# mLSTM heads of a fused block: their results copied off the accumulation bank in one piece, their transposes moved to the shared banks, the gate rows made in two steps, and compressed scores as 64-column products

## The chip, the cores and the metric

The program runs on one core of a Trainium2 chip. The metric is the time of one execution on the device, in microseconds; the median of several runs stands for a kernel. The profile is of one further execution.

## What is computed

The reference chains two transformer blocks over 512 tokens of width 1024, all in float32. Only the first block's attention stage is touched. It projects the normed input into a chunked mLSTM of four heads of width 128 and into a sparse attention ("NSA") of eight heads of width 64, which adds a compressed, a selected and a window branch:

```python
num = inter[..., None] * (qc @ Cs) + Wt @ vc
den = inter * (qc . ns) + sum(Wt)
h   = num / maximum(abs(den), exp(-m))[..., None]      # mLSTM, then rms_norm and a sigmoid gate
s_c = einsum('bgrtd,bgnd->bgrtn', qblk, Kc) - slope * dist_c
p_c = where(valid_c, softmax(s_c), 0)                  # compressed branch, 31 blocks
out = g0 * (p_c @ Vc) + g1 * o_selected + g2 * o_window
```

The gates of the mLSTM are row vectors over the 512 tokens: a cumulative sum of log sigmoids, a running maximum, and an exponential.

## The kernel before

**Arithmetic.** Each float32 operand is split into a high part and a low part (`split`, `split_w`), and a product is made of three matmuls, high x high, low x high and high x low (`mm`, L173 to L175). A weight tile is loaded by DMA (L157), its high part is cast on ACT (L137, `whi`), its low part is made on POOL in four pieces (L147, `wlo`).

**The stage.** `b1_attention` walks a string of step names, `B1_ORDER`, written out by hand. Its steps: `v`, `k`, `q0` to `q3` are the projections of the NSA; `Q`, `V`, `O` those of the mLSTM; `X`, `Y`, `B` make the compressed keys and values; `S` the compressed scores (`b1_cmp_scores`), `T` their transposes; `Ahk` the scores of head h, branch and half k, `Phk` its values, `Eh` its end; `g` the gate projections turned into rows (`b1_gates`), `R` the gate rows (`b1_mlstm_rows`); `M0` to `M3` the mLSTM heads (`b1_mlstm_head`); `W` and `u`/`U` are parts of the output projection and of a side projection that need no result of the later heads. After the stage come the splits of its results (`cat`, L212 and L213) and the rest of the output projection.

The string gives the order in which instructions are written and in which tiles take their buffers. The framework then lists the instructions of each engine in a fixed order of its own; on the chip every engine works through its list in order.

**Banks.** Eight accumulation banks: two "d" (`bankD`, dense projections and much else, tile `psd`), two "t" (transposes of the NSA, `pst`), two "s" (scores, `pss`), one "o" (values, `pso`), one "m" (`bankM`, mLSTM heads only, `psm`).

**An mLSTM head.** `b1_mlstm_head` broadcasts the running maximum through a product with a one-hot column (L1012) and copies it to `mb` (L1014). In two halves p it forms the scores k x q in bank m (L1028, by `mm`), the decay matrix E (L1032 to L1038), their product (L1042, DVE), its high part Wh (L1043, ACT) and low part Wl (L1044, POOL), and the values (L1050 with Wh, L1052 with Wl) for two token tiles, each again in bank m. Columns 0 to 127 of a result hold the low part of the numerator, 128 the denominator, 130 to 257 the high part. ACT copies the low part (L1054), DVE adds the high part out of the bank (L1055), ACT takes the absolute denominator out of the bank (L1056). Then a norm: L1058, L1059 (DVE), four squares (L1063, ACT), two POOL operations (L285, L287), L1065 and four gated scalings (L1068, DVE); each scaling is followed by a transpose on PE (L1070) into bank m, and ACT copies the four transposes (L1072).

**Compressed scores.** For a group of four heads and four token tiles, `b1_cmp_scores` makes 16 results of 32 columns; each is two accumulating products (high and low part of the keys), 32 products in one bank d (L838). One DVE addition of 512 columns adds the bias (L841).

Of the kernel before, what the change touches and what calls it, by code (L numbers as in the profile page):

```python
# [8 lines left out]
AF = mybir.ActivationFunctionType  # L9
OP = mybir.AluOpType  # L10
# [5 lines left out]
NT = 4  # L16
# [24 lines left out]
class Build:  # L41
# [402 lines left out]

    B1_SIZES = dict(k=13, v=1, pa=6, pb=2, mp=6, p2=3, f=2, mf=2, ms=2)
    B1_D = (7,)
    B1_ORDER = "C B0 v B1 Q11 k q0 q1 Q00 X0 X1 g A00 O0 Y0 V0 A10 P00 Y1 S0 A01 A02 Q01 R M0 P01 P02 T0 A03 P03 A12 q2 E0 A11 P10 A13 P11 P12 P13 A30 E1 A20 P20 A21 P21 O1 q3 A22 A23 P22 Q10 A60 P23 V1 E2 A31 S1 P30 P31 A32 T1 A33 P32 M1 c Q21 A40 A42 Q20 P33 u E3 P40 A41 P41 A43 Q30 P42 A50 P43 w E4 W0 A52 P50 A51 P51 P52 A53 P53 A61 E5 A62 Q31 W1 P60 P61 M2 M3 A70 A63 P70 P62 P63 A72 U0 A71 A73 P71 P72 P73 U1 E6 E7"

    def b1_attention(self, ctx, h, first):
        self.c1 = self.pool(ctx, "const1", 1)  # L450
        self.psum(ctx, s=2, o=1, m=1)
        self.pools(ctx, **self.B1_SIZES)
        self.qs, self.mqk, self.mv, self.mo, self.pc = {}, {}, {}, {}, {}
        self.bias, self.part, self.ob = {}, {}, {}
        self.aT, mT, x = [None] * 4, [None] * 4, {}
        for step in self.B1_ORDER.split():
            n = [int(c) for c in step[1:]]
            match step[0]:
                case "v": self.b1_v(h)
                case "k": self.b1_k(h)  # L460
                case "g": self.b1_gates()
                case "q": self.b1_q(h, *n)
                case "C": self.b1_cmp_consts()
                case "B": x["B", n[0]] = self.b1_blocks(h, n[0], first if n[0] else None)
                case "X": x["X", n[0]] = self.b1_compress(n[0], x["B", n[0]])
                case "Y": self.b1_compressed(n[0], *x["X", n[0]])
                case "S": x["S", n[0]] = self.b1_cmp_scores(*n)
                case "T": self.b1_cmp_turn(n[0], x["S", n[0]])
                case "A": self.b1_nsa_scores(*n)
                case "P": self.b1_nsa_values(*n)  # L470
                case "E": self.b1_nsa_end(*n)
                case "R": self.b1_mlstm_rows()
                case "V": self.b1_mlstm_v(h, *n)
                case "O": self.b1_mlstm_o(h, *n)
                case "Q": self.b1_mlstm_qk(h, *n)
                case "w": self.wm = self.split_all(mT[:2], "k", S)
                case "W": self.b1_out(*n)
                case "c": self.b1_conv()
                case "u": self.b1_pT()
                case "U": self.b1_pp(*n)  # L480
                case "M": mT[n[0]] = self.b1_mlstm_head(*n)
        aT = self.aT
        for i in range(4):
            self.show(f"aT{i}", aT[i])
            self.show(f"mT{i}", mT[i])
        return mT[2:] + aT
# [337 lines left out]
    def b1_cmp_scores(self, g):  # L824

        nc, a = self.nc, self.a
        cbias = self.T("f", [128, NT, 128], name="cbias")
        nc.sync.dma_start(cbias, a["c_cbias"][g])
        pc = self.T("f", [128, NT, 128], name="pcx")
        mn = self.smallE([128, NT, 4], "cmn")  # L830
        ls = self.smallE([128, NT, 4], "cls")
        s = self.bankD()
        for i in range(NT):
            for r in range(4):
                hd = 4 * g + r
                lhs = self.qs[hd // 2][:, hd % 2, i * 128:(i + 1) * 128]
                for p in range(2):
                    nc.tensor.matmul(s[:, i * 128 + r * 32:i * 128 + r * 32 + 32], lhs,  # L838
                                     self.kc[:, p, 32 * g:32 * g + 32], start=(p == 0), stop=(p == 1))
        pf = pc.rearrange("p i (r n) -> p i r n", r=4)  # L840
        nc.vector.tensor_tensor(pc, s.rearrange("p (i n) -> p i n", i=NT), cbias, op=OP.add)  # L841
        nc.vector.tensor_reduce(mn, pf, axis=AX.X, op=OP.min)
        nc.vector.tensor_tensor(pf, sub(mn, 0, 128, 0, [[4, NT], [1, 4], [0, 32]]), pf, op=OP.subtract)
        nc.scalar.activation(pc, pc, AF.Exp)
        nc.vector.tensor_reduce(ls, pf, axis=AX.X, op=OP.add)
        nc.vector.reciprocal(ls, ls)
        nc.vector.tensor_tensor(ls, ls, sub(self.gate, 0, 128, 12 * g, [[24, NT], [3, 4]]), op=OP.mult)
        nc.vector.tensor_tensor(ls, ls, sub(self.rmask, 0, 128, 0, [[1, NT], [0, 4]]), op=OP.mult)
        nc.vector.tensor_tensor(pf, pf, sub(ls, 0, 128, 0, [[4, NT], [1, 4], [0, 32]]), op=OP.mult)
        return pc  # L850
# [73 lines left out]
    def b1_mlstm_rows(self):  # L924
        nc = self.nc
        t1 = self.T("mp", [4, S], name="lf1")
        F = self.T("mp", [4, S], name="lfF")

        nc.vector.scalar_tensor_tensor(t1, self.mf, -1.0, self.mf, op0=OP.mult, op1=OP.min)
        nc.scalar.activation(t1, t1, AF.Exp)  # L930
        nc.scalar.activation(t1, t1, AF.Ln, bias=1.0)
        nc.vector.scalar_tensor_tensor(t1, self.mf, 0.0, t1, op0=OP.min, op1=OP.subtract)
        z = sub(self.zero, 0, 4, 0, [[0, S]])
        nc.vector.tensor_tensor_scan(F, t1, z, 0.0, op0=OP.add, op1=OP.add)
        A, nm = self.mi, F
        M = self.T("mp", [4, S], name="mM")
        nc.vector.tensor_sub(A, self.mi, F)
        nc.vector.tensor_tensor_scan(M, A, A, 0.0, op0=OP.max, op1=OP.max)
        nc.vector.tensor_add(nm, F, M)
        nc.scalar.activation(self.rows[32:36], nm, AF.Exp, scale=-1.0)  # L940

        self.m8 = self.C1([128, S], F32R, name="m8")
        self.zeros(self.m8, S)
        lo = self.T("f", [4, S], F32R, name="mlo")
        nc.scalar.copy(self.m8[0:4], M)
        nc.vector.tensor_sub(lo, M, self.m8[0:4].bitcast(F32))
        nc.sync.dma_start(self.m8[4:8].bitcast(F32), lo.bitcast(F32))
        oh = self.smallE([128, 4], "ohraw")
        nc.sync.dma_start(oh, self.a["c_onehot"])
        self.onehot = self.C1([128, 4], F32R, name="onehot")  # L950
        nc.scalar.copy(self.onehot, oh)
        t = self.bankD()
        for i in range(NT):
            nc.tensor.transpose(t[:, i * 128:(i + 1) * 128], self.rows[:, i * 128:(i + 1) * 128], self.ident)
        self.acol = self.C1([128, 2, NT, 4], name="acol")
        for j in range(2):
            nc.vector.tensor_copy(self.acol[:, j], sub(t, 0, 128, 32 * j, [[128, NT], [1, 4]]))
        self.tri = self.C1([128, 128], name="tri")
        nc.sync.dma_start(self.tri, self.a["c_tri"])
# [47 lines left out]
    def b1_mlstm_head(self, hd):  # L1007
        nc = self.nc
        q, k = self.mqk[hd, 0], self.mqk[hd, 1]
        v, mo = self.mv[hd], self.mo[hd]  # L1010
# [4 lines left out]
        num = self.T("mf", [128, NT, 128], name="num")  # L1015
        dn = self.smallE([128, NT], "den")
        for p in range(2):
            T0 = 256 * p
            W = []
            for jp in range(p + 1):  # L1020
                s = self.bankM().rearrange("p (b n) -> p b n", b=2)
                E, Wh, Wl = [self.T("mp", [128, 2, 256], dt, nm) for dt, nm in ((F32, "E"), (F32R, "Wh"), (F32R, "Wl"))]
                W.append((Wh, Wl))
                for b in range(2):
                    j = 2 * jp + b
# [19 lines left out]
            for i in range(2):  # L1045
                ti = 2 * p + i
                o = self.bankM()
                cs = slice(128 * i, 128 * i + 128)
                for j in range(ti + 1):
                    nc.tensor.matmul(o[:, :258], W[j // 2][0][:, j % 2, cs], v[:, j], start=(j == 0), stop=False)  # L1050
                for j in range(ti + 1):
                    nc.tensor.matmul(o[:, 128:258], W[j // 2][1][:, j % 2, cs], v[:, j, 128:], start=False, stop=(j == ti))  # L1052
                lo = self.T("ms", [128, 128], name="nlo")
                nc.scalar.copy(lo, o[:, :128])  # L1054
                nc.vector.tensor_add(num[:, ti], o[:, 130:258], lo)  # L1055
                nc.scalar.activation(dn[:, ti:ti + 1], o[:, 128:129], AF.Abs)  # L1056

        nc.vector.tensor_tensor(dn, dn, self.acol[:, 1, :, hd], op=OP.max)  # L1058
        nc.vector.reciprocal(dn, dn)  # L1059
# [3 lines left out]
            nc.scalar.activation(sc, num[:, ti], AF.Square, scale=dn[:, ti:ti + 1], accum_out=ss[:, ti:ti + 1])  # L1063
        r = self.rstd(ss, MD, [128, NT])
        nc.vector.tensor_mul(r, r, dn)  # L1065
        t = self.bankM()
        for ti in range(NT):
            nc.vector.scalar_tensor_tensor(num[:, ti], num[:, ti], r[:, ti:ti + 1],  # L1068
                                           mo[:, ti], op0=OP.mult, op1=OP.mult)
# [733 lines left out]
```

## Time and profile before

| | before |
|---|---|
| runs, median | 1648.41 us (1645.42 to 1650.79, 3 runs) |
| profiled execution, own time | 1646.16 us |
| its span, first to last instruction | 1644.1 us |
| granted TensorE clock, mean | 0.981 |
| PE busy | 1559.4 us (95%) |
| PE weight loads | 1381.5 us (84%) |
| DVE busy | 962.1 us (59%) |
| ACT busy | 763.5 us (46%) |
| POOL busy | 511.5 us (31%) |
| chain of waits: share of PE / DVE / ACT / DMA / POOL | 76% / 9% / 4% / 4% / 3% |

The stage of the change runs from about 48 us to 333 us of the span. How to read the views: a row of the timeline gives start, duration, engine, line, operation and tile; in brackets stand the engine's idle time before it and what released it. A row of stretches gives the busy time of each engine in that stretch with the number of instructions, then the granted TensorE clock as a share of full speed (1.00 is 2.4 GHz, 0.50 is 1.2 GHz), the DMA share and GB/s. Matmuls overlap: one that lasts 0.28 us can be followed by the next after 0.11 us.

### The profile page before, as it was taken

The numbers are of one execution on the slowest core, as the hardware profiler recorded it, in microseconds if no ns is written. First come the engines' busy times: TensorE is split into PE (matmuls) and PEld (weight loads), VectorE is DVE, ScalarE is ACT, GpSimd is POOL, SyncE is SP. The second block draws the span as 40 slices with busy tenths as digits, with TensorE's granted clock in tenths as the row PEclk, the third lists the DMA queues.
The fourth block names the chain that finished last, engine by engine and source line by source line (L and its number), as shares of the span: only waits on it lengthen the run. The fifth ranks groups of instructions, "written<-read, shape, count | busy, mean of one in ns | idle before, by whom it ended". The sixth has DMA issues, their size and how long they took to land.

```text
span 1644.1 us, 25907 instructions
## 1 busy us (share of the span) xinstructions
PE 1559.4 (95%) x9702; PEld 1381.5 (84%) x9702; DVE 962.1 (59%) x2158; ACT 763.5 (46%) x1727; POOL 511.5 (31%) x645
## 2 busy tenths in 40 slices
PE   6999998889999999899899999999999998999997
PEld 5889977778888888789898899998798887988785
DVE  4486667745444434658866558535468548566453
ACT  4465656734333223545554446433445445554332
POOL 4663533131111112326432243012555340431022
PEclk9999989989999999999999999999999999999999
DMA  5532222455333333322122144135323231332252
GB/s 173 139 106 68 66 78 78 151 184 165 91 101 91 102 110 110 103 89 78 39 74 66 54 117 129 40 105 170 127 62 90 59 89 35 106 115 87 77 180 76
DMA packets 189376, 163.60 MB, mean 100 GB/s; under 512 B 9664, under 2 KB 161312, under 8 KB 189252
## 3 DMA queue, kind: packets, MB, share of 16 engines
q1 hardware_dynamic: 189252, 161.96, 32.7%
q8 instruction: 76, 1.25, 0.3%
q14 instruction: 48, 0.39, 0.1%
HBM read 139.19 MB, written 12.58 MB: 92 GB/s over the span
## 4 chain that ended last, share of the span: by engine, by line
PE 76%; DVE 9%; ACT 4%; DMA 4%; POOL 3%; issue 3%; SPq 0%; POOLq 0%; ACTq 0%; DVEq 0%
PE psd L173 14%; PE psd L174 13%; PE psd L175 13%; PE pss L173 7%; PE pss L174 7%; PE pss L175 7%; POOL wlo L147 1%; PE pss L1447 1%; DMA wraw<-in_w_in_dram 1%; ACT whi L137 1%; PE pst L1472 1%; PE pso L1484 1%; PE pss L1585 1%; DVE pt L202 1%; PE pst L1608 1%
## 5 line engine op out<-in xcount | busy, mean ns | idle before, releaser
L147 POOL TENSOR_TENSOR wlo<-wraw,whi 128x256 fp32r<-128x256 f32 (+1 forms) x384 | 284.4, 772 | 369.1 <-ACT whi L137 353.2
L137 ACT CAST whi<-wraw 128x1024 fp32r<-128x1024 f32 (+2 forms) x215 | 210.9, 982 | 337.3 <-PE psd L174 81.7
L173 PE MATMUL psd<-hh,whi 128*128 128x264 f32 (+2 forms) x1016 | 340.6, 336 | 3.3 <-ACT sg L1671 1.3
L175 PE MATMUL psd<-hh,wlo 128*128 128x264 f32 (+2 forms) x1016 | 338.3, 333 | 0.5 <-DVE wlo L140 0.5
L174 PE MATMUL psd<-hl,whi 128*128 128x264 f32 (+2 forms) x1016 | 338.8, 334 | 0.0
L140 DVE TENSOR_TENSOR wlo<-wraw,whi 128x1024 fp32r<-128x1024 f32 (+1 forms) x118 | 131.2, 1112 | 206.6 <-ACT whi L137 206.5
L173 PEld LDWEIGHTS psd<-hh,whi 128*128 128x128 f32 x1016 | 193.1, 190 | 22.8 <-ACT sg L1671 1.6
L175 PEld LDWEIGHTS psd<-hh,wlo 128*128 128x128 f32 x1016 | 193.2, 190 | 18.3 <-DVE wlo L140 1.0
L174 PEld LDWEIGHTS psd<-hl,whi 128*128 128x128 f32 x1016 | 193.3, 190 | 17.1
L173 PE MATMUL psd<-whi,hh 128*128 128x256 f32 (+1 forms) x480 | 136.6, 286 | 5.1 <-ACT mo L359 2.3
L175 PE MATMUL psd<-whi,hl 128*128 128x256 f32 (+1 forms) x480 | 135.6, 283 | 0.0
L174 PE MATMUL psd<-wlo,hh 128*128 128x256 f32 (+1 forms) x480 | 135.2, 283 | 0.0
L173 PEld LDWEIGHTS psd<-whi,hh 128*128 128x128 f32 x480 | 90.0, 188 | 6.7 <-ACT mo L359 2.5
L330 POOL TENSOR_TENSOR y<-x,g 128x512 f32<-128x512 f32 (+1 forms) x34 | 48.2, 1431 | 145.2 <-DVE x L522 103.2
L201 ACT CAST pt<-pst 128x512 fp32r<-128x512 f32 (+3 forms) x130 | 63.7, 506 | 61.5 <-PE pst L1472 48.1
L202 DVE TENSOR_TENSOR pt<-pst,pt 128x512 fp32r<-128x512 f32 (+3 forms) x130 | 74.7, 583 | 27.9 <-ACT pt L201 27.3
L175 PEld LDWEIGHTS psd<-whi,hl 128*128 128x128 f32 x480 | 90.3, 188 | 0.1
L174 PEld LDWEIGHTS psd<-wlo,hh 128*128 128x128 f32 x480 | 90.2, 188 | 0.2
L1115 POOL TENSOR_TENSOR act<-conv,act 128x512 fp32r<-128x512 f32 x16 | 25.4, 1587 | 161.9 <-ACT act L1114 161.9
L1455 DVE TENSOR_REDUCE gls<-pss 128x1 f32<-128x528 f32 (+1 forms) x66 | 46.5, 704 | 33.8 <-PE pss L1447 33.2
L300 ACT ACTIVATE sq<-x 128x512 f32<-128x512 f32 (+1 forms) x58 | 36.3, 627 | 59.7 <-DVE x L1243 31.5
L175 PE MATMUL pss<-hh,wlo 128*128 128x512 f32 x160 | 63.3, 395 | 0.0
(472 smaller groups left out, 3656.4 us busy)
## 6 DMA issues: line engine op xcount, KB each, us to landing
wraw<-in_w_in_dram SPq DMA_DIRECT2D x108, 512.0 KB
wraw<-in_w_up_dram SPq DMA_DIRECT2D x32, 512.0 KB
wraw<-in_w_out_dram SPq DMA_DIRECT2D x24, 512.0 KB
wraw<-in_w_down_dram SPq DMA_DIRECT2D x16, 512.0 KB
nbias<-in_na_bias_dram SPq DMA_DIRECT2D x16, 408.0 KB
k<-k SPq DMA_DIRECT2D x16, 296.0 KB
wraw<-in_w_ple_gate_dram SPq DMA_DIRECT2D x8, 512.0 KB
x_mid<-x SPq DMA_DIRECT2D x8, 512.0 KB
```

The costliest lines, as they stand in the source:

```text
L137: nc.scalar.copy(hi, raw)
L140: nc.vector.tensor_sub(lo, raw, hi.bitcast(F32))
L147: nc.gpsimd.tensor_sub(lo[:, p[0], p[1]], raw[:, p[0], p[1]], hi[:, p[0], p[1]].bitcast(F32))
L173: m(ps, A[0], B[0], start=start, stop=False)
L174: m(ps, A[0], B[1], start=False, stop=False)
L175: m(ps, A[1], B[0], start=False, stop=stop)
L201: nc.scalar.copy(hi, src)
L202: nc.vector.tensor_sub(lo, src, hi.bitcast(F32))
L300: nc.scalar.activation(sq[:x.shape[0], :x.shape[1]], x, AF.Square, scale=scale, accum_out=ss)
L330: self.nc.gpsimd.tensor_tensor(y[:n, c], x[:, c], g[:n, c], op=OP.mult)
L1115: nc.gpsimd.tensor_sub(lo, u, hi.bitcast(F32))
L1455: nc.vector.tensor_reduce(mx, sv, axis=AX.XY, op=OP.max, negate=True)
```

## The change

Four edits:

- **Result copies.** ACT copies all 258 columns of a head's result to the tile `nlo` at once; the DVE addition and the absolute value read the copy instead of the bank.
- **Transposes.** The four transposes at a head's end go into a bank d instead of bank m.
- **Gate rows.** The step `g` moves to just behind `B1`, the step `R` to just behind `k`, and the last part of `R` (transposes of the rows into columns, `acol`, and the load of `tri`) becomes a step `r` ahead of `S0`.
- **Compressed scores.** Each product now takes the high and low keys side by side, 64 columns; 16 products for a group instead of 32, in two banks d of eight products each. DVE adds the first half with the bias and then the second half, 256 columns each, for each bank.

```diff
-    B1_ORDER = "C B0 v B1 Q11 k q0 q1 Q00 X0 X1 g A00 O0 Y0 V0 A10 P00 Y1 S0 A01 A02 Q01 R M0 P01 P02 T0 ...
+    B1_ORDER = "C B0 v B1 g Q11 k R q0 q1 Q00 X0 X1 A00 O0 Y0 V0 A10 P00 Y1 r S0 A01 A02 Q01 M0 P01 P02 T0 ...
...
+                case "r": self.b1_mlstm_columns()
...
-        s = self.bankD()
-        for i in range(NT):
-            for r in range(4):
-                hd = 4 * g + r
-                lhs = self.qs[hd // 2][:, hd % 2, i * 128:(i + 1) * 128]
-                for p in range(2):
-                    nc.tensor.matmul(s[:, i * 128 + r * 32:i * 128 + r * 32 + 32], lhs,
-                                     self.kc[:, p, 32 * g:32 * g + 32], start=(p == 0), stop=(p == 1))
+        rows = lambda t, b: t[:, 2 * b:2 * b + 2].rearrange("p i (r n) -> p (i r) n", r=4)
+        for b in range(2):
+            s = self.bankD()
+            for j in range(8):
+                i, hd = 2 * b + j // 4, 4 * g + j % 4
+                nc.tensor.matmul(s[:, 64 * j:64 * j + 64].rearrange("p (q n) -> p q n", q=2),
+                                 self.qs[hd // 2][:, hd % 2, i * 128:(i + 1) * 128],
+                                 self.kc[:, :, 32 * g:32 * g + 32], start=True, stop=True)
+            sv = s.rearrange("p (j q n) -> p j q n", j=8, q=2)
+            nc.vector.tensor_tensor(rows(pc, b), sv[:, :, 0], rows(cbias, b), op=OP.add)
+            nc.vector.tensor_tensor(rows(pc, b), sv[:, :, 1], rows(pc, b), op=OP.add)
...
-        nc.vector.tensor_tensor(pc, s.rearrange("p (i n) -> p i n", i=NT), cbias, op=OP.add)
...
+
+    def b1_mlstm_columns(self):
+        nc = self.nc
         t = self.bankD()
...
-                lo = self.T("ms", [128, 128], name="nlo")
-                nc.scalar.copy(lo, o[:, :128])
-                nc.vector.tensor_add(num[:, ti], o[:, 130:258], lo)
-                nc.scalar.activation(dn[:, ti:ti + 1], o[:, 128:129], AF.Abs)
+                lo = self.T("ms", [128, 258], name="nlo")
+                nc.scalar.copy(lo, o[:, :258])
+                nc.vector.tensor_add(num[:, ti], lo[:, 130:258], lo[:, :128])
+                nc.scalar.activation(dn[:, ti:ti + 1], lo[:, 128:129], AF.Abs)
...
-        t = self.bankM()
+        t = self.bankD()
```

The rest of the string is as it was, and no arithmetic outside these functions changes. The order of the instructions on the engines changes throughout the stage. Three places:

**PE, the first head's end (M0).** Names: `mv,Wh` and `mv,Wl` are the values of a head, `mq` its scores, `hh` dense projections, `pt,v` and `k,qs` the NSA, `ident,num` the head's transposes. Before, around the head's four transposes:

```order
L1070 MATMUL psm<-ident,num 128x128
L173 MATMUL psd<-whi,hh 128x256
L174 MATMUL psd<-wlo,hh 128x256
L1070 MATMUL psm<-ident,num 128x128
L175 MATMUL psd<-whi,hl 128x256
L1070 MATMUL psm<-ident,num 128x128
L173 MATMUL psd<-whi,hh 128x256
L174 MATMUL psd<-wlo,hh 128x256
L1070 MATMUL psm<-ident,num 128x128
L175 MATMUL psd<-whi,hl 128x256
```

Dense projections stand between the transposes, as between all of the head's steps. After the change (line numbers of the new file: 1057 and 1059 are the values, 1019 the broadcast for the next head, 1077 the transposes, 860 the transposes of the compressed scores), from the scores of the head's second half on:

```order
L173 MATMUL psm<-mq 128x128
L174 MATMUL psm<-mq 128x128
L175 MATMUL psm<-mq 128x128
L1057 MATMUL psm<-mv,Wh 128x258 x3
L1059 MATMUL psm<-mv,Wl 128x130 x3
L1057 MATMUL psm<-mv,Wh 128x258 x4
L1059 MATMUL psm<-mv,Wl 128x130 x4
L1019 MATMUL psm<-m_743,onehot 128x512
L1077 MATMUL psd<-ident,num 128x128
L860 MATMUL psd<-ident,pcx 128x128 x4
L1077 MATMUL psd<-ident,num 128x128 x3
L920 MATMUL pso<-pct,vc 128x512
```

No dense projection and no product of the NSA stands any more between the head's first scores and its transposes.

**DVE, the same head.** Before, from the division (L1058, L1059) to the gated scalings:

```order
L1058 TENSOR_TENSOR den<-den,acol 128x4
L1059 RECIPROCAL den<-den 128x4
L879 ISA sb,mn<-pss_2191,abias 128x128
L879 ISA mn 128x1
L879 ISA sb,mn<-pss_2196,abias 128x256
L879 ISA mn 128x1
L205 SCALAR_TENSOR_TENSOR qlo<-psd,qs 64x512
```

After the change the same place on DVE (1065, 1066 the division, 1042 the next head's decay matrix, 1072 and 1075 the scalings):

```order
L1049 TENSOR_TENSOR E<-psm,E 128x128
L1062 TENSOR_TENSOR num<-nlo 128x128 x2
L1065 TENSOR_TENSOR den<-den,acol 128x4
L1066 RECIPROCAL den<-den 128x4
L1042 SCALAR_TENSOR_TENSOR E<-mb,acol,tri 128x128 x2
L1072 TENSOR_TENSOR rstd<-rstd,den 128x4
L1075 SCALAR_TENSOR_TENSOR num<-num,rstd,mo 128x128 x4
L202 TENSOR_TENSOR pct<-psd,pct 128x512
L205 SCALAR_TENSOR_TENSOR qlo<-psd,qs 64x512
L926 TENSOR_TENSOR aT<-pso,aT 64x512
L205 SCALAR_TENSOR_TENSOR qlo<-psd,qs 64x512
L360 TENSOR_SCALAR mo<-mo 128x128
```

The work of other steps that stood between is gone from there.

**PE, the end of the stage.** Before, the last values of the NSA and of the head M3, then the rest of the output projection (`cat`):

```order
L1052 MATMUL psm<-mv,Wl 128x130 x4
L907 MATMUL psd<-pt,v 128x256 x3
L907 MATMUL psd<-pt,v 128x128
L916 MATMUL psd<-pct,vc 128x512 x2
L1070 MATMUL psm<-ident,num 128x128 x4
L173 MATMUL pss<-whi,cat 128x512
```

After the change:

```order
L1077 MATMUL psd<-ident,num 128x128
L911 MATMUL psd<-pt,v 128x128
L911 MATMUL psd<-pt,v 128x256 x3
L911 MATMUL psd<-pt,v 128x128
L920 MATMUL psd<-pct,vc 128x512 x2
L173 MATMUL psd<-whi,pT 128x512
```

The 48 products of the side projection (`pT`) that were spread over the last two heads now stand in one piece behind M3's transposes and ahead of `cat`.

## Rows read from the trace of the kernel before

**Rows 1.** The page: busy time of PE, its share of the span, instructions.

```profile
PE 1559.4 (95%) x9702; PEld 1381.5 (84%) x9702; DVE 962.1 (59%) x2158; ACT 763.5 (46%) x1727; POOL 511.5 (31%) x645
```

**Rows 2.** Stretches of the stage: length, PE, PEld, DVE, ACT, POOL, clock, DMA.

```profile
48.00:144.00 96.00, 91.98 (x571) 81.58 (x571) 61.83 (x159) 52.22 (x125) 59.09 (x82) 0.96 0.42 115
144.00:190.00 46.00, 45.80 (x312) 42.10 (x313) 27.20 (x87) 26.96 (x81) 25.14 (x38) 1.00 0.27 78
...
248.00:297.00 49.00, 44.12 (x265) 37.13 (x263) 39.49 (x116) 32.98 (x94) 14.85 (x20) 1.00 0.30 103
297.00:333.00 36.00, 28.69 (x175) 24.43 (x175) 23.42 (x70) 24.58 (x70) 5.17 (x7) 0.94 0.47 162
```

**Rows 3.** Timeline of PE around the first head and its gate rows.

```profile
104.25 0.38 PE L173 MATMUL psd<-whi,hh 128*128 128x256 f32 x1 [2.26 <-ACT mo L359]
...
144.20 0.38 PE L173 MATMUL psm<-mq 128*128 128x256 f32 x1 [0.60 <-ACT mb L1014]
...
189.23 0.27 PE L1070 MATMUL psm<-ident,num 128*128 128x128 f32 x1
...
190.15 0.27 PE L1070 MATMUL psm<-ident,num 128*128 128x128 f32 x1
```

**Rows 4.** Groups by form: the head's operations, mean ns behind the comma.

```profile
L1042 DVE TENSOR_TENSOR E<-psm,E 128x256 f32<-128x256 f32 x8 | 3.3, 418 | 0.5 <-PE psm L175 0.4
...
L1042 DVE TENSOR_TENSOR E<-psm,E 128x512 f32<-128x512 f32 x4 | 2.8, 690 | 5.5 <-PE psm L175 5.5
...
L1054 ACT COPY nlo<-psm 128x128 f32<-128x128 f32 x16 | 4.3, 268 | 5.5 <-PE psm L1052 5.3
...
L1043 ACT CAST Wh<-E 128x256 fp32r<-128x256 f32 x8 | 3.3, 408 | 3.8 <-DVE E L1042 3.8
...
L1014 ACT COPY mb<-psm 128x512 f32<-128x512 f32 x4 | 2.4, 596 | 0.7 <-PE psm L1012 0.7
...
L1044 POOL TENSOR_TENSOR Wl<-E,Wh 128x256 fp32r<-128x256 f32 x8 | 6.1, 764 | 23.7 <-ACT Wh L1043 23.6
L1044 POOL TENSOR_TENSOR Wl<-E,Wh 128x512 fp32r<-128x512 f32 x4 | 5.3, 1322 | 36.9 <-ACT Wh L1043 28.3 <-PE psd L174 8.6
```

**Rows 5.** Timeline of all engines at the last head's end.

```profile
323.63 0.56 PE L1052 MATMUL psm<-mv,Wl 128*128 128x130 f32 x4
...
324.49 1.22 DVE L140 TENSOR_TENSOR wlo<-wraw,whi 128x1024 fp32r<-128x1024 f32 x1 [1.60 <-ACT whi L137]
...
330.96 1.17 PE L1070 MATMUL psm<-ident,num 128*128 128x128 f32 x4 [5.79 <-DVE num L1068]
...
333.32 0.79 PE L173 MATMUL pss<-whi,cat 128*128 128x512 f32 x1 [1.19 <-ACT cat L212]
```

**Rows 6.** Short stretches, columns as in rows 2.

```profile
132.00:137.00 5.00, 5.00 (x18) 4.41 (x18) 4.88 (x12) 2.14 (x6) 0.33 (x1) 0.50 0.39 108
...
206.00:212.00 6.00, 6.00 (x31) 6.00 (x30) 5.90 (x15) 2.56 (x8) 2.23 (x5) 0.50 0.34 113
...
325.00:331.00 6.00, 0.21 (x2) 0.07 (x1) 2.65 (x9) 2.40 (x10) 1.20 (x2) 0.81 0.74 266
...
333.00:339.00 6.00, 5.68 (x14) 4.48 (x15) 3.70 (x6) 2.87 (x6) 0.00 (x0) 0.51 0.49 175
```

**Rows 7.** Groups by form: scores out of their bank, first and last of four widths.

```profile
L879 DVE CUSTOM_DVE_ANT_0 sb<-pss,abias 128x512 f32<-128x512 f32 x16 | 10.9, 682 | 0.0
...
L879 DVE CUSTOM_DVE_ANT_0 sb<-pss,abias 128x128 f32<-128x128 f32 x16 | 4.6, 286 | 9.4 <-PE pst L901 5.7 <-PE pss L878 3.5
```

**Rows 8.** Timeline of PE: 64-column products, and the compressed scores twice.

```profile
126.44 0.28 PE L174 MATMUL psd<-w,grep 128*128 128x64 f32 x1
126.55 0.28 PE L175 MATMUL psd<-w,grep 128*128 128x64 f32 x1
...
127.97 4.51 PE L838 MATMUL psd<-kc,qs 128*128 128x32 f32 x32
...
203.45 4.70 PE L838 MATMUL psd<-kc,qs 128*128 128x32 f32 x32
```

More of the change, by code (lines that the diff above doesn't have):

```diff
@@ L446 @@
     B1_D = (7,)
-    B1_ORDER = "C B0 v B1 Q11 k q0 q1 Q00 X0 X1 g A00 O0 Y0 V0 A10 P00 Y1 S0 A01 A02 Q01 R M0 P01 P02 T0 A03 P03 A12 q2 E0 A11 P10 A13 P11 P12 P13 A30 E1 A20 P20 A21 P21 O1 q3 A22 A23 P22 Q10 A60 P23 V1 E2 A31 S1 P30 P31 A32 T1 A33 P32 M1 c Q21 A40 A42 Q20 P33 u E3 P40 A41 P41 A43 Q30 P42 A50 P43 w E4 W0 A52 P50 A51 P51 P52 A53 P53 A61 E5 A62 Q31 W1 P60 P61 M2 M3 A70 A63 P70 P62 P63 A72 U0 A71 A73 P71 P72 P73 U1 E6 E7"
+    B1_ORDER = "C B0 v B1 g Q11 k R q0 q1 Q00 X0 X1 A00 O0 Y0 V0 A10 P00 Y1 r S0 A01 A02 Q01 M0 P01 P02 T0 A03 P03 A12 q2 E0 A11 P10 A13 P11 P12 P13 A30 E1 A20 P20 A21 P21 O1 q3 A22 A23 P22 Q10 A60 P23 V1 E2 A31 S1 P30 P31 A32 T1 A33 P32 M1 c Q21 A40 A42 Q20 P33 u E3 P40 A41 P41 A43 Q30 P42 A50 P43 w E4 W0 A52 P50 A51 P51 P52 A53 P53 A61 E5 A62 Q31 W1 P60 P61 M2 M3 A70 A63 P70 P62 P63 A72 U0 A71 A73 P71 P72 P73 U1 E6 E7"
     def b1_attention(self, ctx, h, first):
```

## The prediction, made before the changed kernel ran

> **What bounds the kernel now.** I read four views. The page first: PE is busy 95% of the span [rows 1], so the reader is to see that only two things can move the time, PE's own work and the places where PE stands still or runs slowly. Then the stretches between the landmarks of the stage [rows 2], the column of PE beside the length: from 144 to 190 us, where the first mLSTM head runs, PE is busy 45.80 of 46.00 us, although that head needs one bank for a long chain over four engines. Its last four transposes come at 189 to 190 us [rows 3], 45 us after its first product, and nobody waits for them, because dense projections fill PE. The stretches around the later heads are looser: 44.12 of 49.00 and 28.69 of 36.00 us. The timeline at the last head's end [rows 5] shows why: no dense work is left, PE waits 5.79 us for the norm, then 1.19 us for the split of the result. Last, the clock [rows 6]: after the products of 32 columns it is at 0.50 from 132 to 137 us and from 206 to 212 us, with PE busy throughout, and at 0.51 from 333 to 339 us, after the idle end of the last head.
>
> **The change part by part.** All sums are against the profiled execution, 1646.16 us, whose span is 1644.1 us; it lies 2.25 us under the median of 1648.41 us, and I carry the difference over to the median.
>
> *Bank of the transposes, first head: the large cost.* A head's transposes now take a bank d, and banks d are given out in the order of the program. T0, q2 and what follows come behind M0 in that order, so they get a bank d only once M0's first transpose has its own, at the very end of the chain. The order shows the result: between the first scores of M0 and its transposes PE has nothing else, nor has DVE, while before dense products stood between. So M0's chain, hidden before, is bare. Its idle time on PE, hop by hop: first product of E with the scores 0.42, high part 0.41, low parts on POOL 0.76 and about 0.5 for the narrower one [rows 4]: 2.1 us. Three copies of 258 columns, each ahead of the next use of bank m; the trace has 0.27 us for 128 and 0.60 for 512 columns [rows 4], so about 0.38, with the passing on of each 0.45: 1.35 us. The 512-wide product of E between the two score tiles: 0.69 us. The last pair again 2.1 us, more if POOL is still at the 512-wide low part of 1.32 us [rows 4]: 2.7. The end, from the last value to the first transpose, as for M3: 323.63 + 0.56 to 330.96, 6.8 us, less the 1.22 us in which DVE made a weight's low part first [rows 5]: 5.6. Three more transposes (0.9 us apart first to last [rows 3]) and a copy of 0.6 until the next projection has a bank: 1.5. Sum 13.9, say 14 us; the wait before the first product (0.60 us [rows 3]) stays. Bounds: 10 if the pieces overlap, 18 if each hop pays more.
>
> Ahead of M0, the gate columns, both additions of the scores, their softmax, eight small splits of the compressed values, three evictions and four scalings stand on DVE before the low part that M0's scores need: by rows of 0.29 to 0.69 us [rows 4, 7] some 14 us, against 24 dense products at 0.235 us and 35 short ones at 0.11 us, 9.5 us, on PE: 4 us more (0 to 5). After such a halt the clock is low: 6 us at 0.51 behind M3's end [rows 6] lost about 3 us of products. The same behind M0: 3 us.
>
> *Bank of the transposes, second head.* Behind V1 the next dense projections (Q21, Q20) need a bank d after M1's transposes. The order leaves there only NSA steps and M1: on PE 28 score products, 33 transposes, 38 values, 16 compressed scores and 35 products of M1, at 0.11 to 0.23 us about 20.5 us; on DVE eleven evictions, ten scalings and ten splits of mean width, about 0.5 us each (between 0.29 and 0.68 [rows 7]), 16 us, M1's own 6.6 and the second softmax 4.3, together 27 us. DVE ends last: 6 us (bounds 2 and 9).
>
> *End of the stage.* The side projection's 48 products (0.235 us each, 11.3 us) now follow M3 and cover its end and the splits: the idle 5.79 + 1.19 us [rows 5] and the slow clock behind it go. But they no longer fill the last two heads: there DVE has some 24.5 us against 14 us on PE. New: 24.5 + 11.3 + 1 = 37 us; old: 297 to 333.3 us [rows 2, 5] and some 2.6 us lost to the slow clock [rows 6], 39 us. Net -2 us (bounds -8 and +5). Behind M1, Q21 and Q20 come in one piece and out of the looser stretch; of its 4.9 idle us [rows 2] I give half back: -2.5 us.
>
> *Compressed scores.* 32 products took 4.51 and 4.70 us [rows 8], partly at half clock. Products of 64 columns follow each other after 0.11 us [rows 8], so 16 take 1.8 us: -2.7 and -2.9 us. The slow stretches behind them (5.0 us and about 4 us at 0.50 [rows 6]) go if the clock stays up: 2.5 + 2.0 us. I take -9 us of 10.1, since a part falls where DVE ends last; if the clock falls all the same, -5. Four additions of about 0.42 us each instead of one of 0.69 add 1 us of DVE per group, counted in the sums of DVE above.
>
> *Copies and gate rows.* The 16 copies of 258 columns instead of 128 add 0.11 us each on ACT, which is busy 46%: nothing beyond the hops above. The release of bank m comes one DVE addition earlier, which counts only where bank m ends last. The early gate rows take the Exp, Ln and cumulative sums away from the place where PE waited 2.26 us for ACT [rows 3]; what is late next there is DVE, so -2 us. At their new place PE has the broadcast for M0 in its list behind 72 projection products (17 us) and would stand if the rows were later than that. Bounds -2 and +5.
>
> Sum: 14 + 4 + 3 + 6 - 2 - 2.5 - 9 - 2 = +11.5 us: 1657.7 us for a profiled execution, 1660 us for the median.
>
> **A rule against this sum.** What the trace shows of one bank m is the chain of M3 [rows 5]: values, copy, norm, transposes, 6.8 us in which the bank is held. The Trainium skill, page "Perfetto Trace Analysis", section "Optimizing Tensor Performance", says that independent groups of matmuls should rotate through different banks so that the evacuation of one overlaps the products of the next. By that rule, moving the transposes to the pair of banks d is a gain; the sum would be that of the first rival. No row here has a head's transposes in a bank d.
>
> **The rivals.**
>
> *Faster: the heads overlap after all.* If half the bare chain is hidden (7 us in place of the 21 for chain, wait ahead and clock), M1 costs 2 and the end is worth its full -9 us: 7 + 2 - 9 - 2.5 - 9 - 2 = -13.5 us, 1635 us. For it: the idle end of M3 and the slow clock are real and the new order removes them. Against it: the lists of all engines at M0 hold M0 alone. It decides at an idle time of PE in M0 of less than about 5 us.
>
> *No difference.* M0 at its lower bound (10 + 0 + 2), M1 3, the rest as above: 12 + 3 - 15.5 = about 0, 1648 us.
>
> *Much slower: the gate rows come late.* The rows' chain (two cumulative sums, Exp, Ln, about 13 us, then a DMA and the product of it) is behind PE's 17 us in good order only if ACT and DVE reach it at once; every later microsecond stops the whole of PE, as its list has the broadcast ahead of the projections of q0 and q1. With 8 us there: 1668 us. Against it: ACT and DVE are busy only 52.22 and 61.83 of 96 us in that stretch [rows 2].
>
> *It does not do what it says.* Excluded by the order: copies of 258 columns, transposes into `psd`, 64-column products are all there.
>
> **How the numbers follow.** About 0.3%, 5 us, is what a measurement of this kernel can tell from no change. The forecast of 1660 us has 0.52, much slower 0.13: slower 0.65. No difference 0.16. Faster 0.19. The range leaves out about half of the fastest rival and the tail above the slowest: 1635 to 1675 us. It takes in M0 from 10 to 18 us, M1 from 2 to 9, the scores from -10 to -5.
>
> **What would show it.** A stretch of about 20 us around M0 in which PE is busy less than half, with the first transpose waiting more than 4 us for DVE; the same more weakly behind V1, with DVE near full; then no idle time before the first product of `cat`; a clock of 1.00 through the 64-column products. The prediction is wrong if PE stays above 90% through M0, or if the clock falls at the 64-column products too, or if PE stands at the broadcast in the gate rows.

## The result and the profile after

The changed kernel takes 1670.84 us (median of 4 runs, 1667.96 to 1672.69) against 1648.49 us in runs of the kernel before on the same chip: ratio 1.0137, 95% interval 1.012 to 1.0153. It is 22.4 us slower. The forecast was 1660 us, 11.5 us slower, with a range of 1635 to 1675: the side was right, the loss twice the forecast.

The page of the changed kernel, its busy times (compare [rows 1]):

```profile
span 1670.6 us, 25857 instructions
## 1 busy us (share of the span) xinstructions
PE 1572.1 (94%) x9670; PEld 1388.2 (83%) x9670; DVE 964.6 (58%) x2164; ACT 770.5 (46%) x1727; POOL 513.7 (31%) x645
```

The stretches of the kernel before, from 48 us to the first product of `cat`, and from there to the end (length; then busy time of PE, PEld, DVE, ACT, POOL; clock; DMA):

```profile
48.00:333.32 285.32, 265.35 (x1650) 234.00 (x1650) 189.59 (x554) 168.55 (x467) 123.45 (x172) 0.96 0.34 103
333.32:1644.10 1310.78, 1260.77 (x7850) 1118.34 (x7850) 751.48 (x1560) 573.83 (x1208) 367.58 (x442) 0.99 0.32 97
```

The same of the changed kernel, and its stretches around the first head (137 to 171 us, compare [rows 2]) and the last two (318 to 362 us):

```profile
48.00:361.33 313.33, 277.46 (x1619) 238.84 (x1616) 190.30 (x559) 172.65 (x465) 125.97 (x171) 0.91 0.29 86
361.33:1670.60 1309.27, 1259.84 (x7850) 1118.47 (x7850) 753.12 (x1560) 576.04 (x1208) 367.14 (x442) 0.99 0.33 99
...
137.00:150.00 13.00, 11.56 (x45) 9.61 (x45) 8.52 (x29) 4.33 (x11) 1.62 (x3) 0.74 0.15 42
150.00:171.00 21.00, 12.18 (x45) 9.75 (x45) 5.91 (x21) 8.97 (x31) 6.40 (x10) 0.52 0.09 25
171.00:230.00 59.00, 58.16 (x399) 53.24 (x398) 31.83 (x98) 29.08 (x74) 23.49 (x35) 0.97 0.23 61
...
318.00:345.00 27.00, 20.50 (x115) 16.77 (x115) 20.52 (x65) 15.71 (x50) 3.67 (x5) 0.82 0.12 40
345.00:362.00 17.00, 13.35 (x59) 10.35 (x58) 3.84 (x5) 9.08 (x15) 0.00 (x0) 0.99 0.53 179
```

Read the two pairs against each other first. Behind the stage nothing is lost (1309.27 against 1310.78 us). The stage is 28.0 us longer, of which PE's idle time is 15.9 us (313.33 - 277.46 = 35.9 against 20.0) and its busy time 12.1 us, although it has some thirty products fewer: they run at a lower mean clock, 0.91 against 0.96. So nearly half of the stage's loss is not waiting but slow products.

PE's timeline in the first head (brackets: idle time before, and what ended it; L1057 and L1059 are the values, L1061 the copy, L1049 the product with E, L1019 the broadcast for the next head, L1077 the transposes):

```profile
151.82 0.58 PE L1057 MATMUL psm<-mv,Wh 128*128 128x258 f32 x1 [1.01 <-ACT Wh L1050]
...
153.56 0.80 PE L1057 MATMUL psm<-mv,Wh 128*128 128x258 f32 x2 [0.47 <-ACT nlo L1061]
...
157.58 0.58 PE L173 MATMUL psm<-mq 128*128 128x256 f32 x1 [0.78 <-DVE E L1049]
...
159.91 1.01 PE L1057 MATMUL psm<-mv,Wh 128*128 128x258 f32 x3 [0.78 <-DVE E L1049]
161.92 1.23 PE L1057 MATMUL psm<-mv,Wh 128*128 128x258 f32 x4 [0.47 <-ACT nlo L1061]
164.36 0.79 PE L1019 MATMUL psm<-m,onehot 128*128 128x512 f32 x1 [0.47 <-ACT nlo L1061]
169.18 0.47 PE L1077 MATMUL psd<-ident,num 128*128 128x128 f32 x1 [4.02 <-DVE num L1075]
```

Each hop of the chain stands as a wait of PE, with no dense product (`whi,hh`) between. Before, this head lay hidden in 45.80 busy of 46.00 us [rows 2].

The end of the stage, PE and then ACT (compare [rows 5]; `pp` is the side projection, L649 ACT's copies of its results, L212 the split that `cat` needs):

```profile
339.88 0.48 PE L1077 MATMUL psd<-ident,num 128*128 128x128 f32 x1 [1.66 <-DVE num L1075]
...
346.10 0.40 PE L173 MATMUL psd<-whi,pT 128*128 128x512 f32 x1
...
357.28 0.40 PE L175 MATMUL psd<-whi,pT 128*128 128x512 f32 x1
361.33 0.51 PE L173 MATMUL pss<-whi,cat 128*128 128x512 f32 x1 [3.65 <-ACT cat L212]
```

```profile
345.09 0.59 ACT L1079 COPY mo<-psd 128x512 f32<-128x512 f32 x1 [6.25 <-PE psd L1077]
...
356.43 0.60 ACT L649 ACTIVATE pp<-psd 128x512 f32<-128x512 f32 x1 [0.85 <-DMA p_proj<-pp]
357.71 1.05 ACT L137 CAST whi<-wraw 128x1024 fp32r<-128x1024 f32 x1 [0.68 <-PE psd L175]
360.17 0.60 ACT L649 ACTIVATE pp<-psd 128x512 f32<-128x512 f32 x1 [1.41 <-DMA p_proj<-pp]
360.66 1.13 ACT L212 CAST cat<-mo 128x512 fp32r<-128x512 f32 x2
```

The 48 products of the side projection run behind the last head in one piece, 346.10 to 357.68 us, 11.6 us against the 11.3 of the prediction. They stand behind the head's transposes (339.88 us and later), so they cover nothing of the wait ahead of those. And ACT has the eight copies of their results ahead of the split in its list; the last of them waits for a transfer of `pp`. PE waits 3.65 us for the split where it waited 1.19 before.

### The profile page after: what moved, and what is told of

The parts are those of the page before. It is cut to its first block, busy times and chain, and to the rows that moved or that the text cites. A ratio compares the mean times of both kernels' runs of the same rounds, so it can differ in the third digit from the quotient of the medians.

```text
span 1670.6 us, 25857 instructions
## 1 busy us (share of the span) xinstructions
PE 1572.1 (94%) x9670; PEld 1388.2 (83%) x9670; DVE 964.6 (58%) x2164; ACT 770.5 (46%) x1727; POOL 513.7 (31%) x645
## 4 chain that ended last, share of the span: by engine, by line
PE 71%; DVE 9%; DMA 3%; ACT 3%; issue 2%; POOL 1%; SPq 0%; POOLq 0%; ACTq 0%; DVEq 0%
PE psd L173 13%; PE psd L175 12%; PE psd L174 12%; PE pss L173 6%; PE pss L175 6%; PE pss L174 6%; PE pss L1454 2%; PE pst L1479 1%; PE pso L1491 1%; DVE pt L202 1%; PE pss L1592 1%; DMA wraw<-in_w_out_dram 1%; ACT whi L137 1%; PE pst L1615 1%; DVE wlo L140 1%
## 5 line engine op out<-in xcount | busy, mean ns | idle before, releaser
L147 POOL TENSOR_TENSOR wlo<-wraw,whi 128x256 fp32r<-128x256 f32 (+1 forms) x384 | 288.4, 782 | 401.6 <-ACT whi L137 381.3
```

The lines of the kernel that those rows point to most:

```text
L147: nc.gpsimd.tensor_sub(lo[:, p[0], p[1]], raw[:, p[0], p[1]], hi[:, p[0], p[1]].bitcast(F32))
```

## The experiments

Twelve kernels ran beside the changed one. Ratios are to the kernel before, run on the same chip in the same set. Its own median was 1648.4 to 1651.2 us in these sets, so a difference of two medians from different sets is uncertain by 2 to 3 us; where it is small, the ratios decide.

| kernel | median us | ratio (95% interval) |
|---|---|---|
| changed kernel | 1670.84 | 1.0137 (1.012 to 1.0153) |
| all but the bank | 1642.82 | 0.9970 (0.9958 to 0.9983) |
| bank alone | 1695.87 | 1.0296 (1.0280 to 1.0311) |
| scores alone | 1645.10 | 0.9983 (0.9971 to 0.9995) |
| gate rows alone | 1650.01 | 1.0009 (0.9998 to 1.002) |
| first head in d | 1659.66 | 1.0064 (1.0042 to 1.0086) |
| three later heads in d | 1655.28 | 1.0049 (1.0031 to 1.0066) |
| last head in d | 1647.20 | 0.9994 (0.9981 to 1.0007) |
| second head in d | 1641.92 | 0.9953 (0.9935 to 0.9972) |
| bank and copies | 1680.08 | 1.0192 (1.0169 to 1.0215) |
| first head in d, written late | 1647.41 | 0.9987 (0.9975 to 1.0000) |
| first and second in d, late | 1656.03 | 1.0047 (1.0029 to 1.0066) |
| copies and scores | 1640.85 | 0.9949 (0.9931 to 0.9967) |

**All but the bank.** The changed kernel with one line put back:

```diff
-        t = self.bankD()
+        t = self.bankM()
```

> The change with the four transposes of a head back in bank m; copies, gate rows and 64-column scores stay. Theory A (the bank of the transposes cost more than the 22.5 us that the prediction gave it, and the other three parts gave the forecast 11 us): about 1637 us (1633 to 1642), and PE busy over 90% through the first head. Theory B (the bank cost what was forecast, and the other parts gave nothing): about 1648 us (1645 to 1652). Theory C (one of the other parts costs time itself): over 1653 us.

Measured: 1642.82 us. That lies between theories A and B: the bank costs 28.0 us, more than the 22.5 of theory B, and the other three parts gain 5.8 us, half of the 11 of theory A. The sign of theory A is there: from 140 to 186.4 us, in the first head, PE is busy 45.74 of 46.40 us. The stage, and the last head's transposes:

```profile
48.00:327.43 279.43, 260.54 (x1618) 227.92 (x1617) 188.35 (x558) 171.34 (x466) 126.08 (x171) 0.98 0.32 96
```

```profile
314.57 0.59 PE L1077 MATMUL psm<-ident,num 128*128 128x128 f32 x2
```

With the same products, the stage of the changed kernel has 17.0 us more idle time (35.9 against 18.9) and 16.9 us more busy time (277.46 against 260.54). These are two single executions, 32.2 us apart where the medians are 28.0 apart. The last head's transposes wait for nothing here: the 5.79 us of [rows 5] are gone without bank d.

**Bank alone.** The kernel before with `bankM` made `bankD` in that line.

> The kernel before with one edit, the four transposes of a head in a bank d. Theory A: about 1680 us (1675 to 1688), as this part is the whole loss and 11 us of gain are missing beside it. Theory B: about 1671 us (1667 to 1674). Theory C: below 1664 us. In all three PE has less than 60% busy in a stretch of some 20 us around the first head; the clock there is at 0.50 under theory A for 25 us or more.

Measured: 1695.87 us, 47.3 us slower, beyond all theories. What all three had in common is there: from 150 to 170 us PE is busy 11.63 of 20.00 us. So the parts don't add: beside the other three the bank costs 28. The next kernel takes a part of this apart.

**Bank and copies.** The kernel before with the bank and with the copies of 258 columns.

> The kernel before with the transposes in a bank d and the copies of 258 columns. With the bank alone it took 1695.9 us, and PE waited 0.88 us at each release of bank m in the bare heads where the changed kernel waited 0.47. Theory H (the copies pay by these hops alone, at most 4 x 0.41 us in each of four heads): 1689 to 1695 us. Theory K (the copies also bring the rest of the 25 us between the bank alone and the whole change, by another order of the work): 1671 to 1680 us.

Measured: 1680.08 us, so the copies bring 15.8 us here, and theory K stands nearer; it also asked where. The stage and what follows, of the bank alone and then of bank and copies:

```profile
48.00:372.94 324.94, 286.90 (x1651) 249.26 (x1651) 187.95 (x553) 170.38 (x467) 123.84 (x171) 0.89 0.28 82
372.94:1693.20 1320.26, 1266.21 (x7850) 1123.41 (x7850) 751.25 (x1560) 575.46 (x1208) 369.27 (x442) 0.98 0.33 98
```

```profile
48.00:361.06 313.06, 283.00 (x1655) 246.03 (x1653) 186.75 (x554) 173.56 (x467) 124.98 (x172) 0.91 0.30 88
361.06:1681.90 1320.84, 1264.95 (x7850) 1122.61 (x7850) 755.02 (x1560) 574.16 (x1208) 365.56 (x442) 0.98 0.32 97
```

With the copies the stage is as long as in the changed kernel (313.06 against 313.33 us), although this profile and that of the bank alone have a slow clock from 84 to 104 us that cost some 6 us and that the changed kernel's lacks (last section). What is left between these two profiles lies behind the stage: 1320.84 against 1309.27 us, in code that no edit touches. The order of PE's products there differs from kernel to kernel; that this order costs the time is not shown, and the four runs of bank and copies spread over 7 us. In the bank alone PE waits at bank m for the read of the denominator,

```profile
151.85 0.58 PE L173 MATMUL psm<-mq 128*128 128x256 f32 x1 [0.88 <-ACT den L1056]
...
159.04 1.23 PE L1050 MATMUL psm<-mv,Wh 128*128 128x258 f32 x4 [0.88 <-ACT den L1056]
```

0.88 us a release against 0.47 with the copies. Four such hops in a head are 1.6 us; the rest of the 11.9 us in the stage is not told apart.

**Which head.** The changed kernel with bank d for some heads only:

```diff
-        t = self.bankD()
+        t = (self.bankD() if hd in (0,) else self.bankM())
```

and `(1, 2, 3)`, `(3,)` and `(1,)` in place of `(0,)`.

> The changed kernel with the transposes of the first head alone in a bank d, those of the other three back in bank m. With all four back in bank m it took 1642.8 us, with all four in d 1670.8, so the bank costs 28 us there. Theory A (the first head is the loss, 21 us by the prediction and the rest of the 28 too): 1664 to 1670 us. Theory D (the later heads hold most of it): 1650 to 1657 us.

> The changed kernel with the first head's transposes back in bank m and those of the other three heads in a bank d. Theory A: 1643 to 1648 us, since by the prediction's sum the second head costs 6 us and the end gives 4.5 back. Theory D: 1655 to 1663 us, since the second and third heads lose their dense products as the first did and the end gives nothing back.

> The changed kernel with the last head's transposes alone in a bank d. By the prediction's term for the end (the side projection's products cover the wait of 5.8 us and the split behind it, with the slow clock after it): 1635 to 1639 us against 1642.8 with bank m throughout. By theory D (what the side projection fills at the end is missing in the last two heads, where DVE ends last, and the split is late all the same): 1643 to 1650 us.

> The changed kernel with the transposes of the second head alone in a bank d. The three later heads together cost 12.5 us (1655.3 against 1642.8 us with bank m throughout), the last alone 4.4, so 8 us are left for the second and the third. By the prediction's term the second costs 6 us: 1647 to 1651 us. If the loss is the third head's, which the prediction had as a gain of 2.5 us: 1641 to 1645 us. If it lies in both only together: 1644 to 1647 us.

Measured against 1642.82 us with bank m throughout: first head +16.8 us, three later heads +12.5, together 29.3, about the 28.0 of all four. So these two add, and neither theory holds whole: the first head is the larger loss, but less than A had, and the later heads lose where A had them near nothing. Of them the last costs 4.4 us alone, as theory D had it and against a forecast gain; but in the kernel that it is compared with the wait that bank d was to remove is gone already. The second costs nothing that can be measured (-0.9 us, by the ratios -3, their intervals overlapping; forecast +6). That leaves about 9 us for the third head, or for the third with the others; the third alone wasn't run.

Where the 12.5 us lie, from the broadcast for the second head to the first product of `cat`, with bank m throughout and then with three later heads in d:

```profile
192.43:327.43 135.00, 122.43 (x747) 105.10 (x746) 97.70 (x312) 89.99 (x261) 40.55 (x54) 0.99 0.28 91
195.13:344.03 148.90, 130.16 (x747) 109.88 (x745) 99.41 (x313) 90.29 (x261) 40.02 (x54) 0.93 0.25 84
```

The stretch is 13.9 us longer with the same 747 products: PE is idle 6.2 us more, and the products take 7.7 us more at the lower clock.

**Order or sharing.** The gated scalings, the four transposes and their copy of the first head are written as a step of their own, `m0`, behind `q3`; in the second kernel also those of the second head, `m1`, behind `Q20`.

```diff
-... E0 A11 ... O1 q3 A22 ... Q21 A40 A42 Q20 P33 ...
+... E0 A11 ... O1 q3 m0 A22 ... Q21 A40 A42 Q20 m1 P33 ...
...
+                case "m": mT[n[0]] = self.b1_mlstm_turn(*mT[n[0]])
```

> As the kernel with the first head's transposes alone in a bank d (1659.7 us, against 1642.8 with bank m), but its gated scalings and transposes are written later in the program, behind the step q3, so that T0, q2, O1 and q3 get their banks d first; the other heads stay in bank m. Theory A (the loss is the order in which banks d are given out, and not the sharing of the banks): 1642 to 1648 us, PE busy over 90% through the first head. Theory S (the head's transposes in the pair of banks d delay the dense projections wherever they are written): 1653 to 1661 us.

> As the kernel before it in this set, with the second head treated alike: its transposes in a bank d, written behind the step Q20, so that Q21 and Q20 get their banks first. Theory A: 1641 to 1649 us, within 4 us of the kernel with the first head alone. Theory S: 5 us or more above that one. If a head's end in another bank than m really frees the next head: 3 us or more below it, under 1640 us.

Measured: 1647.41 us with the first head, so of its 16.8 us 12.2 go when only the place in the program changes, with the same bank. Theory A holds for it, its sign too (PE busy 38.89 of 40.00 us). The stretch of the first head, in the kernel with the first head in d and then written late:

```profile
150.00:190.00 40.00, 32.10 (x176) 27.89 (x177) 13.99 (x44) 17.25 (x53) 9.10 (x15) 0.74 0.14 36
```

```profile
150.00:190.00 40.00, 38.89 (x261) 34.86 (x261) 19.76 (x56) 22.89 (x61) 20.75 (x33) 1.00 0.24 67
```

261 products instead of 176, at full clock. With the second head also late the time is 1656.03 us, 8.6 us more, against theory A; but the profile places it behind the stage, not in the heads. The part from the first product of `cat` on, with the first head late and then with both:

```profile
338.75:1645.40 1306.65, 1257.52 (x7850) 1115.81 (x7850) 755.01 (x1561) 574.13 (x1208) 368.19 (x442) 0.99 0.33 99
```

```profile
335.49:1651.50 1316.01, 1260.56 (x7850) 1119.94 (x7850) 751.52 (x1561) 574.29 (x1208) 368.81 (x442) 0.98 0.33 98
```

9.4 us more there, again in untouched code and for a reason not found. The two stages are 290.75 and 287.49 us, and only the first of these profiles has the slow clock from 84 to 104 us. So this kernel says nothing sure for or against theory S in the second head.

**Scores alone.** The kernel before with the 64-column products and their four additions.

> The kernel before with one edit, the compressed scores as 64-column products in two banks. Theory A (the edit gives what the prediction took): about 1639 us (1637 to 1644), the clock at 1.00 in the 6 us behind the products. Theory B (the clock falls behind the 64-column products as it did behind those of 32, or what is won there waits for DVE): 1645 to 1649 us.

Measured: 1645.10 us, a gain of 3.5 us: theory B's end. Where the rest went, on PE and in the stretches behind the first and the second group:

```profile
134.00 1.76 PE L838 MATMUL psd<-kc,qs 128*128 128x64 f32 x8 [1.61 <-DVE ls L895]
```

```profile
132.00:134.00 2.00, 0.39 (x3) 0.03 (x1) 1.52 (x6) 0.89 (x3) 2.00 (x3) 1.00 0.86 250
134.00:136.00 2.00, 2.00 (x10) 2.00 (x11) 1.72 (x6) 0.41 (x2) 0.76 (x1) 0.53 0.83 230
...
206.00:208.00 2.00, 2.00 (x20) 1.95 (x19) 1.78 (x7) 2.00 (x8) 2.00 (x4) 1.00 0.01 4
208.00:210.00 2.00, 1.92 (x14) 1.50 (x13) 2.00 (x7) 1.32 (x6) 2.00 (x4) 1.00 0.58 158
210.00:212.00 2.00, 0.84 (x4) 0.40 (x4) 2.00 (x8) 1.18 (x4) 0.63 (x2) 1.00 0.35 123
...
216.00:218.00 2.00, 1.53 (x8) 1.50 (x8) 2.00 (x8) 0.44 (x2) 0.51 (x2) 0.51 0.04 12
```

The products themselves are short, and through the second group the clock holds at 1.00. But PE then stands still behind DVE: 1.61 us ahead of the first group's second half, and from 210 us on, where DVE is busy 2.00 of every 2.00 us. Only then does the clock fall. What was a slow clock with PE busy [rows 6] is now a wait for DVE with the slow clock behind it.

**Gate rows alone.** The kernel before with the new places of `g`, `R` and `r`.

> The kernel before with one edit, the gate rows in two steps with the new places of g, R and r. Theory A: about 1646 us (1644 to 1649), the wait of 2.26 us for the running maximum gone and nothing late in its place. Theory C (the early rows push work of DVE and ACT into a place where PE waits): 1652 us or more.

Measured: 1650.01 us, ratio 1.0009 with 1 in its interval: no measurable change, where -2 us was forecast, and below the 1652 of theory C. The wait of 2.26 us [rows 3], for the output gate `mo` that ACT reached only after the gates' two functions, goes. At the early place of the gates PE waits instead, and from 48 to 72 us its clock is 0.86 where it was 1.00 before:

```profile
48.62 0.60 PE L664 MATMUL psd<-ident,gi 128*4 128x128 f32 x4 [0.77 <-ACT rows L665]
51.07 0.80 PE L173 MATMUL psd<-hh,whi 128*128 128x512 f32 x1 [1.85 <-DVE v L202]
```

**Copies and scores.** The kernel before with these two edits.

> The kernel before with two edits, copies of 258 columns and 64-column scores; gate rows and bank of the transposes as before. If the parts add up (all three but the bank 1642.8 us, gate rows alone 1.4 us slower): 1639 to 1643 us, and the copies are worth 3 to 5 us beside the scores alone at 1645.1. If the copies give nothing where the heads are covered, as the prediction has it: 1644 to 1647 us.

Measured: 1640.85 us, ratio 0.9949: the fastest kernel of the study beside the one with the second head in d (0.9953; their intervals overlap). The copies are worth 4.3 us beside the scores, as the first expectation had it. The last head's transposes in the scores alone, and the end of this kernel, where they wait for nothing and side-projection products stand between them:

```profile
331.25 1.17 PE L1073 MATMUL psm<-ident,num 128*128 128x128 f32 x4 [5.80 <-DVE num L1071]
```

```profile
314.45 0.59 PE L1073 MATMUL psm<-ident,num 128*128 128x128 f32 x2
314.99 0.50 PE L173 MATMUL psd<-whi,pT 128*128 128x512 f32 x1
...
316.49 0.38 PE L1073 MATMUL psm<-ident,num 128*128 128x128 f32 x2
...
327.34 0.50 PE L173 MATMUL pss<-whi,cat 128*128 128x512 f32 x1 [1.51 <-ACT cat L212]
```

The wait of 5.79 us [rows 5] goes with the copies, and with the transposes in bank m. That is the gain that the prediction gave to bank d.

## Why the prediction was right, and where its sizes were wrong

For the first head the mechanism was right: banks d are given out in the order of the program, so dense products leave the head and its chain lies bare. The late-written kernel shows it. For the later heads it was not, and the size of the whole was half. The terms one by one (the measured ones add up to 22.9 us, though the last three were measured without the bank):

| term | forecast us | measured us | from |
|---|---|---|---|
| first head: chain 14, ahead of it 4, clock 3 | +21 | +16.8 | first head in d |
| second head | +6 | about 0 | second head in d |
| third and last head: -2.5 and -2 | -4.5 | +13.4 | later heads less second |
| scores | -9 | -3.5 | scores alone |
| gate rows | -2 | +1.4, not told from 0 | gate rows alone |
| copies | 0 | -4.3 | copies and scores less scores |

- **First head.** The hops were over-counted and the clock under-counted. In 150 to 171 us PE idles 8.8 us, not 14: the end is 4.02 instead of 5.6, the last pair 0.78 instead of 2.7, while copies (0.47 each) and the 512-wide product (0.78) are as forecast. Against this the 12.18 busy us run at 0.52, by which I estimate 12.18 x 0.48 = 5.8 us lost where the sum had 3, and the clock is low ahead of it too (0.74 from 137 to 150 us). Of the 4 us ahead of the head the trace shows 1.10 us of waiting at its first scores, against 0.60 before [rows 3].
- **End of the stage: the step that failed most.** The prediction had the 48 products "follow M3 and cover its end and the splits". They can't cover its end, as they stand behind its transposes in PE's list. The wait of 5.79 us is now 1.66 because transposes of the NSA stand ahead of it, with waits of their own (1.59, 0.37 and 0.46 us from 332 to 338 us), and without bank d it goes whole. That the last two heads lose these products the sum had counted, but at too small a price: PE waits, mostly for DVE, in 318 to 345 us (20.50 busy of 27.00, clock 0.82), then the 11.6 us of the products come on top. And "no idle time before the first product of `cat`" was false: 3.65 us, because ACT's copies of the same 48 products stand ahead of the split. The step looked at PE's list and not at ACT's. How the 13.4 us divide between these two and the third head is not shown.
- **Second head.** The 6 us came from adding up DVE's instructions behind V1 as if all had to end there. Alone, bank d costs this head nothing.
- **Scores.** The clock at 1.00 through the products came true for the second group; "I take -9 us of 10.1" failed, since most of the gain ends in a wait for DVE. The lower bound given, -5, was also too large. In the changed kernel the clock is at 0.50 from 138 to 142 us, in the second half of the first group.
- **Copies.** The prediction named the condition, an earlier release "counts only where bank m ends last", and then gave it 0. It holds at the last head and, where the first head is bare, in its four releases.
- **Gate rows.** The much slower rival did not come about. PE's wait at the broadcast in the gate rows is 0.48 us:

```profile
70.69 0.47 PE L1019 MATMUL psm<-m,onehot 128*128 128x512 f32 x1 [0.48 <-DMA m<-mlo]
```

- **The signs.** The first transpose waits 4.02 us for DVE, as named. PE is busy 58% around the first head, not less than half. The clock falls at the 64-column products of the first group, which the prediction had named as a sign against itself, and it holds through those of the second.

The faster rival needed less than 5 us of idle time in the first head; there were 8.8. The four transposes in a bank d cost 28.0 us, and with the first head written late a bank d is still no faster than bank m (ratios 0.9987 and 0.9970, their intervals overlapping). The Trainium skill, page "Perfetto Trace Analysis", section "Optimizing Tensor Performance", says that independent groups of matmuls should rotate through different banks; here the other banks were already those of the products that had to fill the gap.

That the total came within the range owes something to luck. Inside the bank's sum errors of both signs cancel: the first head was 4 us and the second 6 to 7 us cheaper than forecast, the third and last together 18 us dearer. What was left, the bank 5.5 us dearer than the 22.5 forecast and the other parts gaining 5.8 instead of 11 us, points one way and makes up the miss of 11 us.

## What to carry to other kernels

Before moving a result to a shared pool of banks, ask who takes the next bank of that pool in program order: a tile that fills at the end of a long chain stops all of them, and where it is written can matter more than which bank it has. When filler work is moved to cover one gap, count the gap that it leaves and follow it through every engine's list, its copies on ACT included. Where PE idles, price the slow clock behind it like the idle time itself: of the 28.0 us that the stage grew, 12.1 were busy time of the same or fewer products.

## What was not expected of the hardware

In some executions the clock fell while PE was busy throughout, in the narrow products of the compressed keys. The bank alone, whose program is the same there as that of the kernel before:

```profile
84.00:86.00 2.00, 2.00 (x20) 2.00 (x19) 1.75 (x4) 0.75 (x4) 2.00 (x4) 1.00 0.44 132
86.00:88.00 2.00, 2.00 (x12) 2.00 (x12) 1.39 (x8) 1.57 (x5) 0.81 (x3) 0.52 0.36 52
...
98.00:100.00 2.00, 2.00 (x12) 2.00 (x11) 1.36 (x7) 1.85 (x6) 2.00 (x4) 0.57 0.00 0
```

It stays near 0.50 from 86 to 99 us, some 6 us lost; from 84 to 104 us the mean is 0.66 there and 1.00 in the profile of the kernel before. Profiles of the scores alone, of bank and copies, of the last head in d and of the first head written late show the same (0.66 to 0.71); those of the changed kernel and of all but the bank show 1.00, so that comparison is not touched by it. What decides it was not found. A single profiled span of this kernel is therefore uncertain by some 6 us, and the parts were priced from repeated runs.
